# The indexer's scores block by block of queries, and its top search spread between them

## The chip, the cores and the metric

The kernel runs on one core of a Trainium2 chip. The metric is the device time of one execution in microseconds. The kernel before has a median of 2123.04 us over three runs, from 2120.47 to 2123.62.

## The reference, cut to what matters

A hybrid encoder of two layers on 512 tokens of width 1024, in float32. Layer 0's mixer joins two attentions. The differential one ("b") is four heads with two softmaxes each. The sparse one ("a", eight heads) looks, for each query, only at the 128 keys with the highest indexer scores among the admissible ones:

```
idx_logits = einsum('bqhd,bsd->bqhs', iqb, ik) * IDX_DIM ** -0.5
score = einsum('bqh,bqhs->bqs', iwb, relu(idx_logits))     # 8 indexer heads
score = where(key_chunk <= query_chunk, score, -inf)
_, sel = top_k(score, 128)
```

The softmax of "a" then runs over the selected keys. Around the mixer stand feed-forward layers, and behind it attention to 256 memory tokens.

## The kernel before

Products in float32 precision are made of three matmuls of rounded parts (high by high, high by low, low by high), so each operand is split: ScalarE (ACT) writes the rounded high part, VectorE (DVE) or GpSimd (POOL) the low part. TensorE (PE) executes its instructions in the order of the program text. The other engines' order is set by a planner that simulates the time: what is ready and stands first in the program goes first, weight loads and some other parts have high priority, and `issue_after` puts instructions behind a given one on the same engine.

Queries come in four blocks of 128, i = 0 to 3; a block needs the keys up to its own, (i + 1) x 128. Block 0 has only 128 keys and needs no selection.

In `mixer0` two generators are woven together (`weave`, L79): `gemm` yields after each piece of a projection (six matmuls of 512 columns, counted as 1300), `att` yields the gap that it wants before its next step, and pieces are pulled until the gap is used up. So each step of the attention has a known number of pieces behind it. `None` pulls one piece at a time until something is ready. The pieces are six weight chunks w[0] to w[5] of 16 pieces, then 16 of the memory's keys and values (`mem_kv`), then the output projection (`out_proj`). The last one blocks while the head it needs is not done, and before its second half (`fill`) while the attention is going on (`self.attending`, L661).

The steps of `att` in order: the indexer's keys (`index_keys`), the scores (`index_scores`), the first pair of b heads with top search (`attend_diff`), the second pair, the close of its last head (`close_diff`), four pairs of a heads (`attend64`), which read the masks.

- `index_scores` (L948) takes two indexer heads at a time (j = 0 to 3; z = 0, 1). `split_q` (L745) splits all 512 queries of the pair into `qz` (ACT L751, DVE L752). After a gap of I_QK come, for each z, the products of all three blocks (L788; two of 256, two of 384, two of 512 columns, into three banks "pb" of four), three ReLUs on ACT (L963) and three weighted sums into sc[1] to sc[3] on DVE (L966, L968), and a gap of I_S. At the end DVE marks the inadmissible keys (L972).
- `index_top` (L974) finds the highest scores, eight at a time: 16 rounds for each block, a round being MAX8 (L981) and a load and a replacement of these eight by a marker (L982). It is a generator that goes through the three blocks in turn; at the end it writes the masks `mk` (L986).
- `along` (L1308) runs at each gap of the b heads n rounds of the search (TOP_A = 3 in the first pair, TOP_B = 2 in the second pair and in the close), put behind `self.mark`, the last instruction noted by the step.
- `attend_diff` (L881): transposes and splits of q and k (L742, L761, L752, L767), for each of two softmaxes the products (L788), bias and maximum (DVE L801) and exponential (ACT L802); then both are combined into the weights e (DVE L940). The head's rest is done in the next head's gaps: `transpose_p` (PE L813, ACT L816, DVE L817), products with the values (L896), norm (L905 to L914). In `close_diff` it follows without a gap before the transposes.
- `attend64` ends each head likewise with `transpose_p`, a gap of A_PT = 1950 and eight products (L840).

Of the kernel before, what the change touches and what calls it, by code (L numbers as in the profile page):

```python
# [11 lines left out]
F32 = mybir.dt.float32  # L12
F32R = mybir.dt.float32r
BF = mybir.dt.bfloat16
AF = mybir.ActivationFunctionType
OP = mybir.AluOpType
# [3 lines left out]
P = 128  # L20
# [5 lines left out]
QB = S // P  # L26
# [3 lines left out]
INADMISSIBLE = -3.0e38  # L30
TAKEN = -3.4e38
TAKEN_CUT = -3.2e38
MASK = -float(2.0 ** 99)
# [14 lines left out]
I_1 = 1500  # L48
I_2 = 7150
I_3 = 3900  # L50
I_QK = 2600
I_S = 2600
B_N1 = 1300
B_N2 = 1300
C_N = 0
B_END = 3000
TOP_A = 3
TOP_B = 2
X_K = 2600
WS = (2, 3, 0, 1, 1, 2, 1, 2, 0, 0, 3, 2, 1, 1, 0, 3)  # L60
# [46 lines left out]
class Encoder:  # L107
# [837 lines left out]
        for c in self.unfinished():  # L945
            yield B_END if isinstance(c, str) else c

    def index_scores(self, sc, iq, ikt, coef, mp):  # L948

        nc = self.nc  # L950
        for i in range(1, QB):
            sc[i] = mp.tile([P, (i + 1) * P], F32, name="sc%d" % i, tag="sc%d" % i, bufs=1)
        for j in range(4):
            q = self.split_q(iq[j])
            yield I_QK
            for z in (0, 1):
                h = 2 * j + z
                lg = self.logits(q, ikt, z, blocks=range(1, QB))
                for i in range(1, QB):
                    n = (i + 1) * P  # L960
                    bank, o = lg[i]
                    t = mp.tile([P, n], F32, name="rl%d" % i, tag="e%d" % i, bufs=self.ebufs)
                    nc.scalar.activation(t, bank[:, o:o + n], AF.Relu)  # L963
                    c = coef[:, i * 8 + h:i * 8 + h + 1]
                    if h == 0:
                        nc.vector.tensor_scalar(sc[i], t, c, 0.0, op0=OP.mult, op1=OP.add)  # L966
                    else:
                        nc.vector.scalar_tensor_tensor(sc[i], t, c, sc[i], op0=OP.mult, op1=OP.add)  # L968
                yield I_S
        for i in range(1, QB):  # L970
            n = (i + 1) * P
            nc.vector.memset(sc[i][0:64, n - 64:n], INADMISSIBLE)  # L972

    def index_top(self, masks, sc, mp):  # L974

        nc = self.nc
        for _ in range(16):
            for i in range(1, QB):
                yield
                m8 = self.small.tile([P, 8], F32, name="m8", tag="m8", bufs=4)  # L980
                nc.vector.max(m8, sc[i])  # L981
                nc.vector.match_replace(sc[i], m8, sc[i], TAKEN)  # L982
        for i in range(1, QB):
            n = (i + 1) * P
            mk = mp.tile([P, n], BF, name="mk%d" % i, tag="mk%d" % i, bufs=1)
            nc.vector.tensor_scalar(mk, sc[i], TAKEN_CUT, MASK, op0=OP.is_gt, op1=OP.mult)  # L986
            masks[i] = mk

    def index_gemm(self, banks, src, n, xs):

# [11 lines left out]
    def index_keys(self, out, p, epsv, r, mp):  # L1002
        nc = self.nc
        raw = self.xp.tile([72, S], F32, name="ikraw", tag="sq", bufs=2)
        nc.scalar.copy(raw, p[0:72, :])
        yield I_1
        p = self.bank("pb")
        for i in range(QB):
            nc.tensor.transpose(p[:, i * 72:(i + 1) * 72], raw[:, i * P:(i + 1) * P], self.ident[0:72, 0:72])
        nat = self.xp.tile([P, QB * 72], F32, name="iknat", tag="sq", bufs=2)  # L1010
        nc.scalar.copy(nat, p[:, :QB * 72])
        n3 = nat.rearrange("p (i c) -> p i c", c=72)
        sq = self.xp.tile([P, QB * 64], F32, name="iksq", tag="sq", bufs=2)
        s3 = sq.rearrange("p (i c) -> p i c", c=64)
        nc.scalar.activation(s3, n3[:, :, 0:64], AF.Square)
        ss = self.small.tile([P, 4], F32, name="ikss", tag="ss", bufs=4)
        nc.vector.tensor_reduce(ss, s3, axis=AX, op=OP.add)
        nc.vector.scalar_tensor_tensor(ss, ss, 1.0 / 64, epsv, op0=OP.mult, op1=OP.add)
        f = self.small.tile([P, 4], F32, name="ikf", tag="f", bufs=4)
        self.rsqrt(f, ss, 4)  # L1020
        kn = self.xp.tile([P, QB * P], F32, name="ikn", tag="sq", bufs=2)
        k3 = kn.rearrange("p (i c) -> p i c", c=P)
        for z in (0, 1):
            nc.vector.tensor_mul(k3[:, :, z * 64:z * 64 + 64], n3[:, :, 0:64], f.unsqueeze(2).to_broadcast([P, QB, 64]))
        r2 = self.small.tile([P, 4], F32, name="r2", tag="r2")
        nc.vector.scalar_tensor_tensor(r2, r, (64 ** -0.5) * (8 ** -0.5), r, op0=OP.mult, op1=OP.mult)
        coef = self.small.tile([P, 32 + PAD_SMALL], F32, name="coef", tag="coef", bufs=1)[:, :32]
        nc.vector.tensor_mul(coef.rearrange("p (i h) -> p i h", h=8), n3[:, :, 64:72],
                             r2.unsqueeze(2).to_broadcast([P, QB, 8]))
        yield I_2  # L1030
        p = self.bank("pb")
        for i in range(QB):
            nc.tensor.transpose(p[:, i * P:(i + 1) * P], kn[:, i * P:(i + 1) * P], self.ident)
        g = self.col("l0_idx_k_norm")
        kh = mp.tile([P, S], F32R, name="ikh", tag="ikh", bufs=1)
        nc.scalar.activation(kh, p, AF.Copy, scale=g)
        kl = mp.tile([P, S], F32R, name="ikl", tag="ikl", bufs=1)
        nc.vector.scalar_tensor_tensor(kl, p, g, kh.bitcast(F32), op0=OP.mult, op1=OP.subtract)
        ikt = ((kh, kl), (kh, kl))
        out += [ikt, coef]  # L1040
        yield I_3

    def gain_col(self, q, k, scale):
# [283 lines left out]
    def mixer0(self):  # L1327
        pre, I = "l0_", self.I
        with ExitStack() as ctx:
            self.qkbufs, self.vbufs, self.ebufs = 10, 8, 2  # L1330
            mp = self.open_mixer(ctx, pre)
# [45 lines left out]
                yield from self.mix_out(I[pre + "w_out"], list(range(KB)), os, mp)  # L1377

            def att():
                sc, ik = {}, []  # L1380
                yield from self.wait(ready, 0)
                iq, p, v, r = ready[0]
                yield from self.index_keys(ik, p, v, r, mp)
                yield from self.index_scores(sc, iq, *ik, mp)
                yield from self.wait(ready, 1)
                yield B_N1
                masks = {}
                top = self.index_top(masks, sc, mp)
                yield from self.along(self.attend_diff(*ready[1], 0, gb, "bias0", os[0:2], nlam, sub, mp), top, TOP_A)
                yield from self.wait(ready, 2)  # L1390
                yield B_N2
                yield from self.along(self.attend_diff(*ready[2], 2, gb, "bias0", os[2:4], nlam, sub, mp), top, TOP_B)
                yield from self.along(self.close_diff(), top, TOP_B)
                for _ in top:
                    pass
                yield from self.wait(ready, 3)
                yield from self.attend64(*ready[3], 0, 0, ga, "bias0", os[4:6], mp, masks)
                yield from self.wait(ready, 4)
                yield from self.attend64(*ready[4], 0, 2, ga, "bias0", os[6:8], mp, masks)
                yield from self.unfinished()  # L1400

            self.weave(gemm(), att())
            self.xattn(pre, mp)

# [148 lines left out]
```

## Time and profile before

| | |
|---|---|
| median of three runs | 2123.04 us |
| the profiled execution | 2121.99 us, its span 2120.2 us |
| TensorE busy | 98% of the span |
| VectorE / ScalarE / GpSimd busy | 74% / 54% / 17% |
| the chain that ended last | PE 87%, DVE 7%, ACT 2% |

Times are from the start of the span. The indexer's scores lie at 400 to 443 us, the b heads at 443 to 563, the a heads up to 665. [...] "PEclk" is the clock granted to TensorE as a share of full speed.

### The profile page before, as it was taken

The numbers are of one execution on the slowest core, as the hardware profiler recorded it, in microseconds if no ns is written. First come the engines' busy times: TensorE is split into PE (matmuls) and PEld (weight loads), VectorE is DVE, ScalarE is ACT, GpSimd is POOL, SyncE is SP. The second block draws the span as 40 slices with busy tenths as digits, with TensorE's granted clock in tenths as the row PEclk, the third lists the DMA queues.
The fourth block names the chain that finished last, engine by engine and source line by source line (L and its number), as shares of the span: only waits on it lengthen the run. The fifth ranks groups of instructions, "written<-read, shape, count | busy, mean of one in ns | idle before, by whom it ended". The sixth has DMA issues, their size and how long they took to land.

```text
span 2120.2 us, 32519 instructions
## 1 busy us (share of the span) xinstructions
PE 2083.2 (98%) x12830; PEld 1854.7 (87%) x12834; DVE 1572.0 (74%) x2246; ACT 1136.4 (54%) x1701; POOL 366.6 (17%) x319
## 2 busy tenths in 40 slices
PE   8999999999999999999999999999999999999999
PEld 7989898877788889898979899988888878989997
DVE  8858677589876697685789677684668688958676
ACT  6636344466686565362556354344678566625442
POOL 1101003345431120000020000013453022000000
PEclk9999999999999999999999999999999999999999
DMA  7736535222241166464356466334223225636632
GB/s 228 210 118 183 149 92 179 87 75 70 81 133 64 68 189 170 130 188 129 97 165 176 130 170 178 98 121 150 87 82 130 90 70 149 183 117 186 162 98 92
DMA packets 86122, 279.65 MB, mean 132 GB/s; under 512 B 9681, under 2 KB 12881, under 8 KB 85969
## 3 DMA queue, kind: packets, MB, share of 16 engines
q1 hardware_dynamic: 74448, 235.62, 33.6%
q0 software_dynamic: 11520, 41.95, 11.1%
q8 instruction: 101, 1.65, 0.3%
q14 instruction: 53, 0.43, 0.1%
HBM read 271.24 MB, written 6.29 MB: 131 GB/s over the span
## 4 chain that ended last, share of the span: by engine, by line
PE 87%; DVE 7%; ACT 2%; issue 1%; DMA 1%; POOL 1%; SPq 0%; DVEq 0%; POOLq 0%; ACTq 0%
PE ps_pa L445 26%; PE ps_pa L682 11%; PE ps_pb L445 10%; PE ps_pa L580 10%; PE ps_pb L580 10%; PE ps_pa L633 4%; PE ps_pa L319 2%; PE ps_pb L788 2%; PE ps_pa L1227 2%; PE ps_pb L840 1%; PE ps_pa L1079 1%; PE ps_pb L813 1%; PE ps_pb L633 1%; PE ps_pa L998 1%; DVE wl L159 1%
## 5 line engine op out<-in xcount | busy, mean ns | idle before, releaser
L157 ACT ACTIVATE wh<-wf 128x1024 fp32r<-128x1024 f32 (+2 forms) x211 | 215.3, 1021 | 353.8 <-PE ps_pa L580 121.1
L159 DVE TENSOR_TENSOR wl<-wf,wh 128x1024 fp32r<-128x1024 f32 (+2 forms) x169 | 200.1, 1187 | 49.2 <-ACT wh L157 46.5
L424 DVE TENSOR_TENSOR wl<-s,wh 128x1024 fp32r<-128x1024 f32 x108 | 132.5, 1227 | 51.8 <-ACT wh L423 51.8
L423 ACT ACTIVATE wh<-s 128x1024 fp32r<-128x1024 f32 x108 | 114.3, 1059 | 96.1 <-PE ps_pb L445 34.9
L423 ACT ACTIVATE wh<-wf 128x1024 fp32r<-128x1024 f32 x84 | 88.9, 1058 | 112.8 <-PE ps_pa L445 39.3
L502 POOL DMA_DIRECT2D s<-l_ffn_wq x40 | 35.5, 887 | 538.6 <-ACT s L501 538.6
L159 POOL TENSOR_TENSOR wl<-wf,wh 128x1024 fp32r<-128x1024 f32 x42 | 101.8, 2424 | 142.2 <-ACT wh L157 140.6
L682 PE MATMUL ps_pa<-wh,xh 128*128 128x512 f32 x384 | 123.4, 403 | 0.0
L682 PE MATMUL ps_pa<-wh,xl 128*128 128x512 f32 x384 | 119.9, 394 | 0.0
L682 PE MATMUL ps_pa<-wl,xh 128*128 128x512 f32 x384 | 119.4, 392 | 0.0
L475 POOL DMA_DIRECT2D s<-l_ffn_wq x40 | 35.6, 890 | 443.3 <-DMA s<-l_ffn_wq 297.8
L424 DVE TENSOR_TENSOR wl<-wf,wh 128x1024 fp32r<-128x1024 f32 x84 | 102.5, 1220 | 8.0 <-ACT wh L423 5.1
L590 DVE TENSOR_TENSOR dn<-ps_pa,R 128x512 f32<-128x512 f32 x48 | 33.1, 689 | 89.4 <-PE ps_pa L580 89.0
L224 POOL TENSOR_TENSOR acc<-acc,sq 128x512 f32<-128x512 f32 (+1 forms) x37 | 54.1, 1462 | 246.2 <-ACT sq L223 245.0
L580 PE MATMUL ps_pb<-hh,wl 128*128 128x512 f32 x352 | 96.3, 392 | 0.0
L580 PE MATMUL ps_pb<-hh,wh 128*128 128x512 f32 x352 | 96.2, 392 | 0.0
L580 PE MATMUL ps_pb<-hl,wh 128*128 128x512 f32 x352 | 96.2, 392 | 0.0
L580 PE MATMUL ps_pa<-hh,wl 128*128 128x512 f32 x328 | 89.5, 392 | 0.0
L580 PE MATMUL ps_pa<-hl,wh 128*128 128x512 f32 x328 | 89.4, 391 | 0.0
L580 PE MATMUL ps_pa<-hh,wh 128*128 128x512 f32 x328 | 89.4, 391 | 0.0
L590 DVE TENSOR_TENSOR dn<-ps_pb,R 128x512 f32<-128x512 f32 x48 | 33.0, 688 | 73.4 <-PE ps_pb L580 73.0
L682 PEld LDWEIGHTS ps_pa<-wh,xl 128*128 128x128 f32 x384 | 72.7, 189 | 16.1
(377 smaller groups left out, 5950.1 us busy)
## 6 DMA issues: line engine op xcount, KB each, us to landing
wf<-l_ffn_wq SPq DMA_DIRECT2D x120, 512.0 KB, 3.4
s<-l_ffn_wq SPq DMA_DIRECT2D x80, 512.0 KB, 4.5
s<-l_ffn_wq POOLq DMA_DIRECT2D x80, 512.0 KB, 6.7
wf<-l_ffn_wd SPq DMA_DIRECT2D x64, 512.0 KB, 3.8
wf<-l_w_in SPq DMA_DIRECT2D x48, 512.0 KB, 3.2
wf<-l_ffn_wd SPq DMA_DIRECT2D x32, 384.0 KB, 3.0
wf<-l_mem_wkv SPq DMA_DIRECT2D x16, 512.0 KB, 3.2
wf<-l_w_out SPq DMA_DIRECT2D x16, 512.0 KB, 3.2
```

The lines of the kernel that those rows point to most:

```text
L157: self.leading = nc.scalar.activation(wh[:, sl], w[:, sl], AF.Copy)
L159: eng.tensor_sub(wl[:, sl], w[:, sl], wh.bitcast(F32)[:, sl])
L224: self.summed = (eng or nc.gpsimd).tensor_add(acc[:, :n], acc[:, :n], sq[:, :n])
L319: nc.tensor.matmul(p, w[a][:, k * P:(k + 1) * P], xs[k][c], start=k == order[0] and a == c == 0, stop=k == order[-1] and a == 1)
L423: self.leading = nc.scalar.activation(h, t, AF.Copy)
L424: self.parted = nc.vector.tensor_sub(l, t, h.bitcast(F32))
L445: self.nc.tensor.matmul(bank[:, sl], w[a][:, o:o + P], xs[k][b], start=first and z == a == b == k == 0, stop=z == a == 1 and k == KB // 2 - 1,
L580: self.nc.tensor.matmul(bank, w[a][:, j * P:(j + 1) * P], h, start=j == a == e == 0, stop=j == nb - 1 and (a, e) == ops[-1])
L590: nc.vector.tensor_mul(t, bank, f.R)
L633: nc.tensor.matmul(banks[dd], a[:, o:o + P], parts(k)[b], start=k == first and a is wh and b == 0, stop=k == last and a is wl)
L682: nc.tensor.matmul(banks[i], xs[k][a][:, i * P:(i + 1) * P], w[b][:, kk * 512:kk * 512 + 512], start=k == a == b == 0, stop=k == KB - 1 an ...
L788: nc.tensor.matmul(bank[:, o:o + n], a, b[:, :n], start=c == 0, stop=c == len(ops) - 1)
```

## The change

The scores are summed block by block: all eight indexer heads for block 1, then for block 2, then for block 3. Each step (i, j) needs the split of only 128 queries, which `index_query` makes one step ahead, into two buffers for each z. A step's product goes to one bank. The search of block 1 (16 rounds) is run between the sums of block 2, two rounds behind each sum; eight rounds of block 2 run between the sums of block 3, one behind each. What is left (eight rounds of block 2, 16 of block 3) runs as before along the b heads, with TOP_A = 2. The rounds of one block follow one another, where the three blocks took turns; a block's mask is written behind its last round. The gaps of the scores are new.

```diff
-I_QK = 2600
-I_S = 2600
+I_S = ((1300, 1300), (2600, 1300), (1300, 1300))
+I_TOP = (0, 2, 1)
-TOP_A = 3
+TOP_A = 2
...
+    def index_query(self, q, i, mp):
+        nc, out = self.nc, []
+        for z in (0, 1):
+            mine, other = slice(z * 64, z * 64 + 64), slice(64 - z * 64, 128 - z * 64)
+            t = mp.tile([P, P], F32R, name="iqz%d" % z, tag="iqz%d" % z, bufs=2)
+            src = q[mine, i * P:(i + 1) * P]
+            nc.scalar.copy(t[mine, :], src)
+            nc.vector.tensor_sub(t[other, :], src, t.bitcast(F32)[mine, :])
+            out.append(t)
+        return out
+
+    def index_scores(self, masks, iq, ikt, coef, mp):
+        nc = self.nc
+        kh, kl = ikt
+        tops = []
+        todo = [(i, j) for i in range(1, QB) for j in range(4)]
+        nxt = self.index_query(iq[0], 1, mp)
+        for c, (i, j) in enumerate(todo):
+            n = (i + 1) * P
+            if j == 0:
+                sc = mp.tile([P, n], F32, name="sc%d" % i, tag="sc%d" % i, bufs=1)
+            q = nxt
+            if c + 1 < len(todo):
+                i2, j2 = todo[c + 1]
+                nxt = self.index_query(iq[j2], i2, mp)
             for z in (0, 1):
                 h = 2 * j + z
...
+                p = self.bank("pb")
+                for k in (kh, kl):
+                    nc.tensor.matmul(p[:, :n], q[z], k[:, :n], start=k is kh, stop=k is kl)
+                t = mp.tile([P, n], F32, name="rl%d" % i, tag="e%d" % i, bufs=self.ebufs)
+                nc.scalar.activation(t, p[:, :n], AF.Relu)
+                g = coef[:, i * 8 + h:i * 8 + h + 1]
+                if h == 0:
+                    self.mark = nc.vector.tensor_scalar(sc, t, g, 0.0, op0=OP.mult, op1=OP.add)
+                else:
+                    self.mark = nc.vector.scalar_tensor_tensor(sc, t, g, sc, op0=OP.mult, op1=OP.add)
+                with self.tc.issue_after(self.mark.ins):
+                    for _ in range(I_TOP[i - 1]):
+                        next(tops[-1], None)
+                yield I_S[i - 1][z]
+            if j == 3:
+                nc.vector.memset(sc[0:64, n - 64:n], INADMISSIBLE)
+                tops.append(self.index_top(masks, sc, i, mp))
+        self.top = (c for top in tops for c in top)
...
+    def index_top(self, masks, sc, i, mp):
+        nc = self.nc
+        n = (i + 1) * P
+        for c in range(16):
+            m8 = self.small.tile([P, 8], F32, name="m8", tag="m8", bufs=4)
+            nc.vector.max(m8, sc)
+            nc.vector.match_replace(sc, m8, sc, TAKEN)
+            if c == 15:
+                mk = mp.tile([P, n], BF, name="mk%d" % i, tag="mk%d" % i, bufs=1)
+                nc.vector.tensor_scalar(mk, sc, TAKEN_CUT, MASK, op0=OP.is_gt, op1=OP.mult)
+                masks[i] = mk
+            yield
...
             def att():
...
-                yield from self.index_scores(sc, iq, *ik, mp)
+                yield from self.index_scores(masks, iq, *ik, mp)
+                top = self.top
```

## Rows read from the trace of the kernel before

**Rows 1.** The page: busy time, share of the span, instructions.
```profile
PE 2083.2 (98%) x12830; PEld 1854.7 (87%) x12834; DVE 1572.0 (74%) x2246; ACT 1136.4 (54%) x1701; POOL 366.6 (17%) x319
```

**Rows 2.** Busy time by stretch: PE, weight loads, DVE, ACT, POOL, PEclk, DMA share, GB/s.
```profile
400.80:443.40 42.60, 42.60 (x199) 35.81 (x198) 33.85 (x49) 27.60 (x49) 18.06 (x11) 1.00 0.22 75
443.40:563.00 119.60, 111.17 (x548) 92.75 (x547) 110.08 (x298) 70.95 (x144) 55.44 (x35) 0.96 0.21 71
```

**Rows 3.** Waits of PE, 360 to 660 us: total, times, longest.
```profile
PE ps_pb L813 <- DVE e L940: 6.6, 7, 2.9
```

**Rows 4.** Busy time in slices of 10 us, same columns.
```profile
470.00:480.00 10.00, 7.89 (x41) 6.26 (x42) 9.85 (x24) 2.91 (x7) 10.00 (x7) 1.00 0.28 100
...
500.00:510.00 10.00, 7.38 (x24) 5.61 (x25) 9.88 (x21) 2.81 (x5) 7.37 (x6) 0.66 0.17 53
...
540.00:550.00 10.00, 8.21 (x45) 6.82 (x43) 9.99 (x34) 6.49 (x19) 3.41 (x2) 1.00 0.11 36
550.00:560.00 10.00, 8.35 (x36) 6.86 (x37) 8.93 (x23) 3.14 (x6) 2.55 (x2) 0.83 0.11 44
```

**Rows 5.** Busy time in slices of 2 us, same columns.
```profile
504.00:506.00 2.00, 2.00 (x9) 1.90 (x10) 1.92 (x5) 1.31 (x3) 1.28 (x1) 0.50 0.00 0
```

**Rows 6.** Timeline of PE: start, duration, instruction, idle time before.
```profile
404.59 0.63 PE L682 MATMUL ps_pa<-wh,xh 128*128 128x512 f32 x2
...
407.34 0.28 PE L788 MATMUL ps_pb<-ikh,qz 128*128 128x256 f32 x1
...
408.39 0.63 PE L682 MATMUL ps_pa<-wh,xh 128*128 128x512 f32 x2
...
551.11 0.63 PE L813 MATMUL ps_pb<-ident,e 128*128 128x128 f32 x2 [2.89 <-DVE e L940]
...
655.72 0.39 PE L840 MATMUL ps_pb<-pz0h,vp 128*128 128x512 f32 x1
...
657.00 1.25 PE L813 MATMUL ps_pb<-ident,e 128*128 128x128 f32 x10
658.01 0.48 PE L633 MATMUL ps_pa<-oh,wh 128*128 128x512 f32 x1
```

**Rows 7.** Timeline of DVE, same columns.
```profile
403.67 0.69 DVE L693 TENSOR_REDUCE ss<-sq 128x8 f32<-128x512 f32 x1 [0.73 <-ACT sq L691]
404.39 0.23 DVE L696 TENSOR_SCALAR ss<-ss,epsv 128x8 f32<-128x8 f32 x1
...
454.80 1.48 DVE L981 MAX8 m<-sc 128x8 f32<-128x512 f32 x3
...
457.31 0.54 DVE L982 MATCH_REPLACE8 sc<-m,sc 128x384 f32<-128x384 f32 x1
...
547.66 1.01 DVE L981 MAX8 m<-sc 128x8 f32<-128x512 f32 x2
...
550.61 1.94 DVE L940 SCALAR_TENSOR_TENSOR e<-e,w,e 128x128 f32<-128x128 f32 x4
...
659.55 0.55 DVE L817 TENSOR_TENSOR pz2l<-ps_pb,pz2h 128x384 fp32r<-128x384 f32 x1
```

**Rows 8.** Groups of DVE instructions by line: count, busy us, mean ns, idle before.
```profile
L968 DVE SCALAR_TENSOR_TENSOR sc<-rl,coef,sc 128x256 f32<-128x256 f32 (+2 forms) x21 | 15.5, 783 | 3.1 <-ACT rl L963 3.1
L752 DVE TENSOR_TENSOR qz<-qk,qz 64x512 fp32r<-64x512 f32 x6 | 5.8, 971 | 0.2
...
L981 DVE MAX8 m<-sc 128x8 f32<-128x512 f32 x16 | 10.9, 681 | 0.0
L982 DVE MATCH_REPLACE8 sc<-m,sc 128x512 f32<-128x512 f32 x16 | 10.8, 673 | 0.0
L981 DVE MAX8 m<-sc 128x8 f32<-128x256 f32 x16 | 6.6, 412 | 0.1
L982 DVE MATCH_REPLACE8 sc<-m,sc 128x256 f32<-128x256 f32 x16 | 6.5, 406 | 0.0
L982 DVE MATCH_VALUE_LOAD sc<-m,sc 128x8 f32 x48 | 3.7, 76 | 0.1
```

More of the change, by code (lines that the diff above doesn't have):

```diff
@@ L946, in close_diff @@
             yield B_END if isinstance(c, str) else c
-    def index_scores(self, sc, iq, ikt, coef, mp):
-        nc = self.nc
[L951 to L955, printed above, removed]
+    def index_query(self, q, i, mp):
[8 more added lines that the diff above has]
+        return out
@@ L956, in index_scores @@
             for z in (0, 1):
                 h = 2 * j + z
[L958 to L974, printed above, removed]
-        nc = self.nc
[L977 to L987, printed above, removed]
+                p = self.bank("pb")
@@ L1038, in index_keys @@
         nc.vector.scalar_tensor_tensor(kl, p, g, kh.bitcast(F32), op0=OP.mult, op1=OP.subtract)
-        ikt = ((kh, kl), (kh, kl))
-        out += [ikt, coef]
+        out += [(kh, kl), coef]
         yield I_3
@@ L1379, in att @@
             def att():
-                sc, ik = {}, []
+                ik, masks = [], {}
                 yield from self.wait(ready, 0)
@@ L1383, in att @@
                 yield from self.index_keys(ik, p, v, r, mp)
-                yield from self.index_scores(sc, iq, *ik, mp)
+                yield from self.index_scores(masks, iq, *ik, mp)
+                top = self.top
                 yield from self.wait(ready, 1)
                 yield B_N1
-                masks = {}
-                top = self.index_top(masks, sc, mp)
                 yield from self.along(self.attend_diff(*ready[1], 0, gb, "bias0", os[0:2], nlam, sub, mp), top, TOP_A)
```

## The prediction

> **What bounds the kernel now.** Read first the busy times: TensorE (PE) is busy for 2083.2 of 2120.2 us, 98% [rows 1]. A kernel in this state gets shorter only where PE waits or runs at a lower clock, so I look for such places near the change. The busy times by stretch give the two that it touches [rows 2]. While the indexer's scores are summed (400.8 to 443.4 us) PE is busy for all of 42.60 us, at full clock, and VectorE (DVE) for 33.85. In the difference attention behind it (443.4 to 563.0) PE is busy for 111.17 of 119.60 us at a mean clock of 0.96, and DVE for 110.08. That second stretch is short of DVE, and it is where the 48 rounds of the top search (a search for eight maxima, a load of them, a replacement) run today. The list of waits says what PE waits for: the transposes of the weights e wait for DVE's line 940 seven times, 6.6 us together [rows 3]. Slices of 10 us place them [rows 4]: PE is idle for 2.11 us in 470 to 480, 2.62 in 500 to 510, 1.79 and 1.65 in 540 to 560. In 500 to 510 the granted clock falls to 0.66, in 550 to 560 to 0.83. [...] Sum: 8.2 us idle and 5.1 us of clock. These 13.3 us are all that the change can win.
>
> **What it changes for PE.** Nothing in amount: 48 score products as before, of the same 256, 384 and 512 columns, with the same tiles as weights. No DMA is added. Only the place of projection pieces shifts. A piece is six matmuls, (407.34 - 404.59) / 2 = 1.375 us, and six score products take 408.39 - 407.34 = 1.05 us [rows 6]. Before, the gaps of the scores pull 4 x (2 + 2 + 2) = 24 pieces; afterwards 4 x 2 + 4 x 3 + 4 x 2 = 28, so every later step of the attention comes four pieces later in the projections.
>
> **The end of the mixer: +1.3 us.** Counting every gap, the attention pulls 132 pieces today from the first of w[0] on, and 134 can be pulled before out_proj blocks on `attending`. Afterwards it wants 136: the last gap, behind the last head's transposes, gets none of its two. Today those transposes start at 657.00, from 658.01 two pieces follow [rows 6], and DVE has the last lower part written at 659.55 + 0.55 = 660.10 [rows 7]. Without pieces the eight products, 657.00 - 655.72 = 1.28 us at the head before [rows 6], can't end before about 660.6, where 658.0 + 1.28 = 659.3 would be free of waits. Below stands 0 (another wait absorbs it), above 2 x 1.375 = 2.75; I take 1.3. The rest of that head lies beside the four pieces of `fill`.
>
> **DVE in the scores: +1 us, between 0 and 10.4.** Block 1's 16 rounds move in here, each 0.412 + 0.076 + 0.406 = 0.894 us, and eight of block 2's, which lie between that and block 3's 0.681 + 0.076 + 0.673 = 1.430, so 1.16 [rows 8]. That is 14.3 + 9.3 = 23.6 us. The splits of the queries become 24 of 64x128 in place of 8 of 64x512. A search of 512 columns takes 0.269 us longer than one of 256, 1.05 ns for a column; 384 fewer columns take 0.4 off the 0.97 us of a split [rows 8], which leaves 0.3 to 0.57 each: no loss to 6 us, I take 1. With 1 us for the four added pieces' weights DVE has 33.9 + 23.6 + 2 = 59.5 us of work in a stretch that grows to 28 x 1.375 + 8 x 1.05 = 46.9 us. So 12.6 us don't fit. If the searches wait and the rest is served, PE notices nothing (0). If the queue is in program order, the split for step c + 2 stands behind the searches of step c. A step of block 2 then costs DVE 4 x 0.894 for rounds, 2 x 0.783 for sums [rows 8], 0.7 for two splits and, by estimate, 1.0 for the projections' share (33.85 us less 24 sums and 6 splits is 9.2, 0.22 for each us of PE): 6.9 us, beside 4.8 us of PE (three pieces, four products). A step of block 3, with two rounds of 1.16, costs 5.4 beside 3.7. Four of each leave 8.4 + 6.8 = 15.2 us, less one step's lead of 4.8: 10.4. I take a value near the low end, since today's rows show how a round's halves are ordered: the three searches come first, from 454.80, and the replacements after them, that of block 2 at 457.31 [rows 7], not search and replacement of one block in turn. What has to wait for its predecessor lets another through. With one block at a time each half-round waits for the one before, so splits and sums slip between.
>
> **DVE in the difference attention: -2 us, between -8.1 and +4.** Today every gap of the first pair of heads brings one round of each block, three in all, 0.894 + 1.16 + 1.43 = 3.5 us. Afterwards it brings two, of block 2 (2.3 us) and then of block 3 (2.9 us); the first four gaps of the second pair bring 2.9 where 2.3 stood. So the share for each gap falls by 1.2 and 0.6 us and then rises by 0.6, and what didn't fit into the scores is still to be done here. The two waits concerned cost 2.11 and 2.62 + 3.4 = 8.1 us together [rows 4]. All may go; or the 12.6 us left over may deepen them, which I bound by half as much again, 4. The first pair's rounds fall from 24 x 1.16 = 27.9 us to 8 x 1.16 + 8 x 1.43 = 20.7, 7.2 less, against 12.6 left over; but late rounds stop PE only where an instruction that it needs stands behind them. I take a quarter of what is lost there, 2.
>
> The extra order between rounds has a price too. Three independent searches take 1.48 us, where their durations add up to 1.64 (0.412, 0.681 and the mean of the two for the middle one); a dependent pair, reduce and scale, starts 0.03 us after the first one's end (404.39 against 403.67 + 0.69) [rows 7]. A step in a chain so loses some 0.1 us, 48 x 2 x 0.1 = 9.6 us at most if nothing slips between, 0 if something always does. This is inside the bounds above.
>
> [...]
>
> **The closing wait: -4.7 us.** At 551.11 PE has waited 2.89 us for line 940 [rows 6], which starts at 550.61 behind two searches (1.01 us from 547.66) [rows 7] and two replacements. The idle time of this place is 1.79 + 1.65 and its clock 1.7, 5.1 us [rows 4]. Afterwards 8 rounds are left after the first pair's 16, at two a gap: they end in the fourth gap of the second pair, and nothing of them is queued here. The two searches and two replacements, of 512 and 256 columns, are about 1.0 + 0.67 + 0.41 = 2.1 of the 2.95 us between 547.66 and 550.61 [rows 7, 8], and rounds stand ahead of these too. The wait falls to some 0.4 us, at which the clock holds: a wait of 2.11 us in 470 to 480 did not lower it [rows 4]. Bounds: 0 (the leftover arrives here) and 5.1. What is late next is line 1302's, which stays.
>
> ScalarE gets 24 small copies for 8, in a stretch with 27.60 of 42.60 us busy [rows 2]: nothing. The masks come earlier and are used later.
>
> **Sum.** -4.7 - 2 + 1 + 1.3 = -4.4 us. The profiled execution took 2121.99 us (span 2120.2), which gives 2117.6; the median of the runs is 1.05 us higher at 2123.04. On it I predict 2118.6 us.
>
> **Rivals.**
> A, everything smooths: the leftover is served in gaps and all 13.3 us go, less 1.3: -12, 2111. For it: after 563 DVE has slack, and in the chain nothing starves. Against it: DVE's work up to the end of the search is longer than PE's.
> B, the load only moves: the first two waits stay, the scores cost 2, the closing wait keeps half: -2.5 + 2 + 1.3, +0.8, 2123.8. For it: 2.9 us in a gap against 3.5 is little.
> C, slower: in the scores the splits stand behind the searches, 10.4 us, with the closing wait gone and the end paid: 10.4 + 1.3 - 5.1 = +6.6, 2129.6. It decides from the point at which a split starts after PE has used up the step before. For it: 59.5 us of work in 46.9. Against it: the order of the halves [rows 7].
>
> **Chances.** Forecast 0.45, of its own range 2114 to 2122; A 0.20; B 0.21; C 0.14. A measurement of this kernel tells 0.2%, 4.2 us, from no change: faster is below 2118.8, slower above 2127.3. Of the forecast I count half as faster and half as same: faster 0.23 + 0.20 + 0.01 = 0.44, same 0.22 + 0.17 = 0.39 (part of B), slower 0.14 + 0.03 = 0.17. The range, 2110.5 to 2128, takes in A's time and most of C's.
>
> **What will show it.** Right: the wait for line 940 near the close is under 1 us, and the clock there 1.00; PE stays busy in the scores; a wait of about 1.3 us for line 817 stands at the last head, ahead of `fill`. Wrong: PE waits in the scores for the new splits by more than 2 us (C), the slices of the first pair lose more than 8.1 us (B), or the rounds run on into the second head of the second pair, so that the closing wait stays.

## The result: slower by 15 us, outside the range

The changed kernel has a median of 2138.18 us over five runs (2135.74 to 2140.77), against 2123.04: a ratio of 1.0073, 95% interval 1.0058 to 1.0088. Forecast were 2118.6, between 2110.5 and 2128.0. The chance given to slower was 0.17.

The first matmul of the attention to the memory tokens, right behind layer 0's mixer, places the loss. This is that line in the profiled execution before (start of the first and the last, us), and after it the same matmul afterwards (now L1248):

```profile
L1227 PE MATMUL ps_pa<-xh,wh x32: 389/389/478, 679.5 to 701.3; 128*128 128x512 f32 x32
```

```profile
L1248 PE MATMUL ps_pa<-xh,wh x32: 389/389/478, 692.3 to 714.0; 128*128 128x512 f32 x32
```

The mixer takes 12.8 us more, of 17.3 that the profiled execution is longer. Of the rest, 3.4 us come at 1600 to 1800 us, where this execution ran at a mean clock of 0.98, for 1.00 before, with the same waits.

PE's work is what it was. Busy time of the changed kernel on the page [rows 1], then by stretch, up to the end of the search and the second pair and for the rest of the mixer, in the kernel before and in the changed one:

```profile
PE 2089.8 (98%) x12830; PEld 1856.6 (87%) x12834; DVE 1589.6 (74%) x2262; ACT 1137.5 (53%) x1717; POOL 366.9 (17%) x319
```

```profile
380.00:570.00 190.00, 181.57 (x879) 150.98 (x878) 155.19 (x365) 108.31 (x207) 81.15 (x51) 0.97 0.22 75
570.00:690.00 120.00, 117.92 (x621) 97.14 (x624) 88.00 (x182) 88.63 (x177) 39.72 (x36) 1.00 0.31 100
```

```profile
380.00:570.00 190.00, 175.07 (x828) 143.31 (x827) 165.87 (x371) 103.71 (x211) 77.06 (x48) 0.96 0.21 72
570.00:690.00 120.00, 114.79 (x605) 93.75 (x608) 83.47 (x174) 84.89 (x173) 40.72 (x35) 1.00 0.30 97
```

PE has as many matmuls. Of its 6.6 us more of busy time some 5 are, by estimate, the lower clock: a slice's length times what its clock is short of 1.00, summed over slices of the whole span, is 10.2 us, where it was 5.3. DVE is busy for 17.6 us more. PE is idle for 14.93 us up to 570, where it was for 8.43, and for 5.21 behind that, where it was for 2.08. The slices of 10 us that lose most of the changed kernel [rows 4], same columns:

```profile
430.00:440.00 10.00, 6.42 (x24) 4.63 (x23) 9.76 (x21) 4.95 (x10) 2.52 (x1) 0.90 0.27 96
440.00:450.00 10.00, 10.00 (x42) 8.12 (x41) 9.63 (x25) 3.94 (x7) 2.41 (x1) 0.93 0.07 19
...
460.00:470.00 10.00, 7.68 (x38) 6.10 (x37) 9.70 (x26) 7.03 (x13) 4.31 (x3) 1.00 0.15 52
480.00:490.00 10.00, 7.31 (x29) 5.32 (x28) 9.80 (x14) 3.77 (x6) 5.70 (x4) 0.79 0.15 53
490.00:500.00 10.00, 10.00 (x49) 8.59 (x49) 9.80 (x26) 4.11 (x10) 0.59 (x1) 0.87 0.17 54
...
510.00:520.00 10.00, 8.11 (x39) 6.29 (x38) 9.84 (x19) 4.53 (x8) 7.20 (x7) 0.99 0.15 52
520.00:530.00 10.00, 10.00 (x48) 8.58 (x47) 9.80 (x24) 4.04 (x10) 4.53 (x3) 0.84 0.31 107
...
540.00:550.00 10.00, 6.50 (x29) 4.72 (x28) 9.79 (x16) 4.45 (x7) 2.54 (x1) 1.00 0.15 55
...
560.00:570.00 10.00, 9.46 (x50) 7.73 (x49) 5.74 (x21) 5.60 (x16) 3.56 (x3) 1.00 0.24 79
```

The number behind the comma is PE's busy time (what is missing to 10 is idle), the third number behind the comma is DVE's, and the third from the end is PE's clock. DVE is busy for 9.6 to 9.8 us in every one of them but the last, 560 to 570, which is shown for the closing wait. What PE waits for, 360 to 700 us (total, times, longest) [rows 3]:

```profile
PE ps_pa L682 <- DVE vp L727: 7.1, 4, 2.3
PE ps_pa L1100 <- POOL wl L159: 3.2, 2, 2.4
PE ps_pb L788 <- DVE m L801: 2.8, 2, 2.0
PE ps_pb L813 <- DVE e L940: 2.6, 6, 0.7
PE ps_pb L813 <- DVE qz L752: 2.1, 2, 1.3
```

The wait for line 940 is down from 6.6 to 2.6 us. At the head of the list stands one that the kernel before does not have: the projection itself (L682) waits for its own banks, which DVE frees when it writes the low part of the values (L727). Where, in PE's timeline [rows 6]:

```profile
433.73 0.73 PE L682 MATMUL ps_pa<-wh,xh 128*128 128x512 f32 x2 [1.29 <-DVE vp L727]
...
438.14 1.22 PE L682 MATMUL ps_pa<-wh,xh 128*128 128x512 f32 x2 [2.30 <-DVE vp L727]
...
544.92 0.73 PE L682 MATMUL ps_pa<-wh,xh 128*128 128x512 f32 x2 [1.86 <-DVE vp L727]
548.22 0.73 PE L682 MATMUL ps_pa<-wh,xh 128*128 128x512 f32 x2 [1.64 <-DVE vp L727]
...
567.62 0.33 PE L813 MATMUL ps_pb<-ident,e 128*128 128x128 f32 x1 [0.20 <-DVE e L940]
568.28 0.98 PE L813 MATMUL ps_pb<-ident,e 128*128 128x128 f32 x7 [0.34 <-DVE e L940]
```

The last two are the closing wait: 0.54 us in all, at full clock. The first two lie in the scores, the next two beside the weights e of the third head. What DVE does ahead of the second, and GpSimd beside it:

```profile
433.98 0.61 DVE L987 SCALAR_TENSOR_TENSOR sc<-rl,coef,sc 128x384 f32<-128x384 f32 x1
434.62 2.35 DVE L956 TENSOR_TENSOR iqz<-qk,iqz 64x128 fp32r<-64x128 f32 x1
437.00 0.43 DVE L1003 MAX8 m<-sc 128x8 f32<-128x256 f32 x1
437.35 0.73 DVE L727 SCALAR_TENSOR_TENSOR vp<-ps_pa,r,vp 128x512 fp32r<-128x512 f32 x1
```

```profile
434.31 2.52 POOL L159 TENSOR_TENSOR wl<-wf,wh 128x1024 fp32r<-128x1024 f32 x1 [5.75 <-ACT wh L157]
```

A split of 0.28 us takes 2.35: it ends just after GpSimd's low part of a weight, which runs from 434.31 to 436.83. The values stand behind it and a search, and PE behind the values.

The largest such stretch lies further on, in the difference attention. There the four operations of line 940, which take 1.94 us where GpSimd has only a memset of 0.15 us beside them [rows 7], take 5.59 beside three GpSimd operations:

```profile
479.39 5.59 DVE L940 SCALAR_TENSOR_TENSOR e<-e,w,e 128x128 f32<-128x128 f32 x4
```

```profile
479.28 1.04 POOL L700 TENSOR_TENSOR qk<-qk,f 128x512 f32<-128x512 f32 x1
480.28 2.44 POOL L159 TENSOR_TENSOR wl<-wf,wh 128x1024 fp32r<-128x1024 f32 x1
482.68 1.22 POOL L700 TENSOR_TENSOR qk<-qk,f 128x512 f32<-128x512 f32 x1
```

Added up over the whole kernel, the 16 operations of line 940 take 16.0 us, for 11.2 before, and the 32 of line 696 (in the norm of the heads) 16.9, for 12.6. The splits of the queries take hardly more than before: 24 small ones 9.7 us, where eight large ones took 9.4.

Such stretches were in the kernel before, too. Its weighted sums, minimum, median and maximum in ns:

```profile
L968 DVE SCALAR_TENSOR_TENSOR sc<-rl,coef,sc x21: 472/620/2465, 410.1 to 440.2; 128x256 f32<-128x256 f32 x7, 128x384 f32<-128x384 f32 x7, 128x512 f32<-128x512 f32 x7
```

The mean of 783 ns that the prediction used [rows 8] hid it: half of the sums take 0.62 or less, one took 2.465. The mean of 0.97 us for a split hid it too: of those six, half take 0.69 or less and two 1.54. There DVE had time to spare, busy for 33.85 of 42.60 us [rows 2].

### The profile page after: what moved, and what is told of

Read it like the earlier page. It is cut to its first block, busy times and chain, and to the rows that moved or that the text cites. A ratio compares the mean times of both kernels' runs of the same rounds, so it can differ in the third digit from the quotient of the medians.

```text
span 2137.5 us, 32557 instructions
## 1 busy us (share of the span) xinstructions
PE 2089.8 (98%) x12830; PEld 1856.6 (87%) x12834; DVE 1589.6 (74%) x2262; ACT 1137.5 (53%) x1717; POOL 366.9 (17%) x319
## 4 chain that ended last, share of the span: by engine, by line
PE 59%; DVE 3%; ACT 1%; issue 0%; DVEq 0%
PE ps_pa L445 19%; PE ps_pa L580 8%; PE ps_pb L445 8%; PE ps_pb L580 7%; PE ps_pa L682 6%; PE ps_pa L633 2%; PE ps_pa L319 1%; PE ps_pa L1248 1%; PE ps_pb L840 1%; PE ps_pa L1100 1%; PE ps_pb L788 1%; PE ps_pb L813 1%; PE ps_pb L633 1%; DVE wl L159 1%; PE ps_pb L319 1%; DVE xl L207 0%
## 5 line engine op out<-in xcount | busy, mean ns | idle before, releaser
L682 PE MATMUL ps_pa<-wh,xh 128*128 128x512 f32 x384 | 124.5, 406 | 7.1 <-DVE vp L727 7.1
L682 PE MATMUL ps_pa<-wh,xl 128*128 128x512 f32 x384 | 121.3, 398 | 0.0
L682 PE MATMUL ps_pa<-wl,xh 128*128 128x512 f32 x384 | 120.5, 395 | 0.7 <-POOL wl L159 0.7
L682 PEld LDWEIGHTS ps_pa<-wl,xh 128*128 128x128 f32 x384 | 73.2, 191 | 18.0 <-POOL wl L159 1.6
```

The lines of the kernel that those rows point to most:

```text
L682: nc.tensor.matmul(banks[i], xs[k][a][:, i * P:(i + 1) * P], w[b][:, kk * 512:kk * 512 + 512], start=k == a == b == 0, stop=k == KB - 1 an ...
```

## The experiments

Each ratio is against the kernel before, run in the same series on the same chip (medians of before there: 2122.65 to 2124.64 us), with its 95% interval; it differs from the quotient of the medians by up to 0.0007. No interval reaches further than 0.0016 to either side, so a difference of two ratios is uncertain by some 0.0015 to 0.002. Three theories were set against each other first: the place of the rounds on DVE, the chain of dependent half-rounds, and the phase (every later step comes four pieces later).

**e1_chain**, the search alone block after block, same gaps, scores as before.

```diff
-        for _ in range(16):
-            for i in range(1, QB):
+        for i in range(1, QB):
+            for _ in range(16):
```

> The kernel before, its scores untouched; only the top search takes its 48 rounds block after block (16 of block 1, then 16 of block 2, then 16 of block 3) in the same gaps of the difference attention, three and then two a gap, where it took the three blocks in turn. So each half-round depends on the one before. Three theories of the 15 us. Place: what costs is where the rounds stand on VectorE (in the scores and beside the values of w[1], so that the projection's own banks come free late); it expects no change here, 2123 within 4 us. Chain: the dependence itself costs some 0.1 us a step, 96 steps; it expects 2131 or more. Phase: the four pieces by which every later step comes later cost it; it expects 2123 here, as place does.

Measured: 2119.67 us, 0.9977 (0.9966 to 0.9987). No cost of the chain shows; the order gains. The first pair gets lighter rounds, which may be the reason and is not shown to be: line 940 is also less stretched in its first two heads (2.69 and 1.94 us, for 3.68 and 2.71). PE's idle time falls from 2.11 to 0.79 us in 470 to 480 and from 2.62 to under 0.25 in 500 to 510 (there the clock loss of 3.4 goes too); the wide rounds come late, and the closing wait grows to 4.94 us.

**e2_shift**, the phase alone.

```diff
-I_QK = 2600
+I_QK = 3900
```

> The kernel before with I_QK 3900 for 2600: each of the four steps of the scores pulls one piece of the projection more, 28 for 24, so that every later step of the attention comes four pieces later, as in the changed kernel. Scores, splits and search stay as before. Phase expects most of the 15 us here: 2133 or more. Place and chain expect 2123 to 2126 (the last head's lost two pieces, 1.3 us, are in this one too).

Measured: 2132.07 us, 1.0038 (1.0025 to 1.0051). Phase is a cause, worth about half of the loss. Its waits [rows 3 for before], PE's timeline and GpSimd's:

```profile
579.28 0.65 PE L913 MATMUL ps_pb<-ident,orr 128*128 128x128 f32 x4 [1.82 <-POOL orr L244]
...
585.80 0.50 PE L1079 MATMUL ps_pa<-wl,mh 128*128 128x512 f32 x1 [1.97 <-POOL wl L159]
```

```profile
574.50 1.64 POOL L244 TENSOR_TENSOR f<-ss,mhalf 128x8 f32<-128x8 f32 x1
576.10 1.97 POOL L700 TENSOR_TENSOR qk<-qk,f 128x512 f32<-128x512 f32 x1
578.04 1.18 POOL L244 TENSOR_TENSOR orr<-ov,mhalf 128x4 f32<-128x4 f32 x1
579.20 3.23 POOL L244 TENSOR_TENSOR f<-ss,mhalf 128x8 f32<-128x8 f32 x2
...
583.40 2.35 POOL L159 TENSOR_TENSOR wl<-wf,wh 128x1024 fp32r<-128x1024 f32 x1
```

The last head's inverse root (orr) is now queued behind the norm of the heads of w[5], and the memory weights' low part behind both. Before, the root came first:

```profile
566.40 1.01 POOL L244 TENSOR_TENSOR orr<-ov,mhalf 128x4 f32<-128x4 f32 x1 [6.92 <-DVE ov L907]
```

By the gaps, its step followed the 13th of the 16 pieces of w[5] before and follows the first piece of the memory's weights now: four pieces carry it past the end of w[5].

**e3_no_rounds_in_scores**, the changed kernel with the search as before.

```diff
-TOP_A = 2
+TOP_A = 3
...
-                with self.tc.issue_after(self.mark.ins):
-                    for _ in range(I_TOP[i - 1]):
-                        next(tops[-1], None)
```

> The changed kernel with its scores block by block of queries and the 28 pieces, but no round in the scores: the search takes the three blocks in turn in the difference attention, as before (three rounds a gap, then two). Left from the change: the order of the scores, the 24 small splits and the shift by four pieces. Place expects it near the kernel before: 2121 to 2127. Chain expects the same (the turns are back). Phase expects 2133 or more, since the shift is still there.

Measured: 2131.01 us, 1.0035 (1.0022 to 1.0048), the same as e2 and with the same waits. So beside the shift the new order of the scores adds nothing that shows.

**e4_24_pieces**, the changed kernel without the shift.

```diff
-I_S = ((1300, 1300), (2600, 1300), (1300, 1300))
+I_S = ((1300, 1300), (1300, 1300), (1300, 1300))
```

> The changed kernel with I_S (1300, 1300) for block 2 too: 24 pieces in the scores for 28, so no shift; the rounds stay in the scores, in four pieces' less time. Phase expects the time of before, 2123 to 2127. Place expects no gain, 2138, or worse by up to 4 us, since the same VectorE work has 5.5 us less of the scores to stand beside. Chain expects 2138.

Measured: 2130.46 us, 1.0028 (1.0017 to 1.0039): between what phase and place expected. Both count, and add up to the change (0.38 or 0.35, and 0.28, against 0.73%). Among PE's waits, 360 to 700 us, stands now that of rival C, for the new splits:

```profile
PE ps_pb L980 <- DVE iqz L956: 2.2, 2, 1.5
```

**e6_blocks_24**, e4 with its 24 rounds moved out of the scores.

```diff
-I_TOP = (0, 2, 1)
+I_TOP = (0, 0, 0)
-TOP_A = 2
+TOP_A = 3
```

> The changed kernel with 24 pieces in the scores (I_S 1300 throughout) and none of the rounds in them: I_TOP (0, 0, 0), TOP_A 3, the search block after block as in e1_chain. It is e1_chain with the scores in the new order and the 24 small splits, and e4_24_pieces with the 24 rounds moved out of the scores. Theory rounds (the rounds in the scores hold up what stands behind them on VectorE): 2119 to 2122, as e1_chain, some 10 us below e4_24_pieces. Theory splits (the new order of the scores and its small splits cost by themselves): 2126 or more.

Measured: 2123.3 us, 0.9999 (0.9991 to 1.0008). Moving the rounds out of the scores takes off e4's 0.29% (6 us). Against e1 the new order and the small splits cost some 0.2%, so neither theory holds whole.

**e8_low_on_dve**, the changed kernel with the low parts of w[2] on DVE. From 425 to 450 us GpSimd then has nothing to do, and DVE more.

```diff
-WS = (2, 3, 0, 1, 1, 2, ...
+WS = (2, 3, 0, 0, 1, 2, ...
```

> The changed kernel with the four low parts of w[2] computed on VectorE (WS[3] 0 for 1) in place of GpSimd: 4 x 1.21 = 4.8 us more work for VectorE in the scores, but no GpSimd operation beside them. In the changed kernel a split of 0.28 us took 2.35 and sums of 0.6 to 0.7 took up to 2.8 while GpSimd worked on such a low part. Theory collision (those stretched operations are what the values and the splits wait for): faster than the changed kernel by 2 to 5 us, 2133 to 2136. Theory amount (VectorE has too much to do, whatever stands beside it): slower by 2 to 5 us, 2140 to 2143.

Measured: 2131.0 us, 1.0031 (1.0019 to 1.0042), 0.42% (8.9 us) below the changed kernel, with 4.9 us more of low parts on DVE. (The sums that the expectation speaks of took up to 2.38 us, not 2.8.) The same place in its timeline of DVE:

```profile
433.00 0.73 DVE L727 SCALAR_TENSOR_TENSOR vp<-ps_pa,r,vp 128x512 fp32r<-128x512 f32 x1
433.65 0.61 DVE L987 SCALAR_TENSOR_TENSOR sc<-rl,coef,sc 128x384 f32<-128x384 f32 x1
434.29 0.28 DVE L956 TENSOR_TENSOR iqz<-qk,iqz 64x128 fp32r<-64x128 f32 x1
...
434.95 0.74 DVE L727 SCALAR_TENSOR_TENSOR vp<-ps_pa,r,vp 128x512 fp32r<-128x512 f32 x1
```

The split takes 0.28 us, and the second part of the values comes 1.95 us behind the first, where it was 4.41 (432.94 to 437.35). From 420 to 460 us PE loses 0.8 us of idle time and clock, for 5.3; from 460 to 560 it loses 11.6, for 15.9. Only the first of these two gains is traced to operations: behind 460 line 940 is as stretched as ever (15.1 us in all). An edit that moves the low parts could also have won by having the weights ready earlier; but in the changed kernel PE never waits for those of w[2].

**e9_before_low_on_dve**, the control.

> The kernel before with the four low parts of w[2] on VectorE (WS[3] 0 for 1), as e8_low_on_dve did to the changed kernel, where it took some 9 us off. This is its control. Theory collision (the gain of e8 is undoing what the change brought: two-input operations of VectorE on GpSimd's work in a stretch that the change filled up): the kernel before has 8.75 us of VectorE slack in its scores, so nothing to gain, 2121 to 2126. Theory general (the four low parts stand better on VectorE in any case): 2112 to 2118.

Measured: 2123.59 us, 0.9999 (0.9991 to 1.0008). What e8 gained is undoing something that the kernel before does not pay.

**e11_24_low_on_dve**, both undone: e4 with the same WS.

> The changed kernel with both: 24 pieces in its scores (no shift, e4_24_pieces took some 9 us off) and the low parts of w[2] on VectorE (e8_low_on_dve took some 9 us off). If shift and collision are two causes that add up and are the whole loss: 2138 - 9 - 9 = 2120, 2118 to 2124. If the amount of VectorE work is a third cause (the scores are four pieces shorter here and VectorE has 4.8 us more to do): 2127 or more.

Measured: 2123.6 us, 0.9997 (0.9988 to 1.0006). Undoing the two edits, the shift and the low parts of w[2] on GpSimd, takes back the whole loss:

| scores of the changed kernel | low parts of w[2] on GpSimd | on DVE |
|---|---|---|
| 28 pieces | 1.0073 | 1.0031 |
| 24 pieces | 1.0028 | 0.9997 |

The shift is worth 0.34 to 0.45%, the collision with these low parts 0.31 to 0.42%, equal within the noise. What remains of the change is neither faster nor slower than the kernel before, though e1 shows that the order of its rounds alone gains 0.23%.

These are two edits and not two separate mechanisms. All 16 operations of line 940 together, in us:

| before | changed | e8 | e4 | e11 | e2 |
|---|---|---|---|---|---|
| 11.2 | 16.0 | 15.1 | 9.2 | 9.5 | 9.6 |

So in the changed kernel the four pieces bring collisions of their own, at line 940, which go with the pieces (e4, e11) and not with e8's edit. And yet e2, the same shift in the kernel before, costs 0.38% without them. What a shift meets depends on what else has moved.

**e10_chain_low_on_dve** and **e12_chain_all_low_on_dve**, e1 with the low parts of w[2], and of w[2] and w[3], on DVE (WS[3], and WS[3] and WS[4], 0).

> e1_chain (search block after block, scores as before) with the low parts of w[2] on VectorE. Theory collision: as e1_chain, 2118 to 2122. Theory general: 2108 to 2114, and then it beats both kernels.

> e1_chain with the low parts of w[2] and of w[3] on VectorE (WS[3] and WS[4] 0). Those of w[3] are used in the difference attention, where VectorE is busy 9.5 of 10 us: 4 x 1.21 = 4.8 us more work for it there. Theory amount: slower than e10_chain_low_on_dve by 3 to 8 us. Theory collision: within 2 us of it, since what VectorE takes on it gets back from stretched operations.

Measured: 2120.95 us, 0.9983 (0.9974 to 0.9992), and 2128.24 us, 1.0018 (1.0009 to 1.0026). e10 is e1 again. In e12 DVE is too full: PE waits 5.6 us for the last mask (L986). So here taking over GpSimd's work paid only where DVE got back more than it took.

**e5_shift_two**, **e16_shift_two_in_scores**, a shift of two pieces, made in two ways.

```diff
-I_QK = 2600
+I_QK = 3900
-B_N1 = 1300
-B_N2 = 1300
+B_N1 = 0
+B_N2 = 0
```

```diff
-            yield I_QK
+            yield I_QK + 1300 * (j < 2)
```

> The kernel before with I_QK 3900 (four pieces later, as e2_shift) and B_N1 and B_N2 at 0 for 1300: one piece given back ahead of each pair of heads, so that from the second pair on the attention comes two pieces later than before, not four. The square root of the closing head (orr, on GpSimd) then stands ahead of the factors of the heads of w[5] in GpSimd's queue again; in e2_shift it stood behind them and the memory weights' low part behind both. Theory order (the price of the shift is that place in GpSimd's queue, a step and no slope): 2123 to 2126. Theory slope (each piece of shift costs the same, some 2 us): 2128.

> The kernel before with one piece more in the first two steps of the scores only (I_QK 3900 for two of four): a shift by two pieces with every gap of the difference attention as before. The closing head's square root then stands behind one of the four factors of w[5]'s heads, for three in e2_shift. Theory step (what counts is the place in GpSimd's queue): 2122 to 2125. Theory slope (each piece costs the same): 2127 to 2129.

Measured: 2138.36 us, 1.0065 (1.0049 to 1.008), and 2128.45 us, 1.0027 (1.0016 to 1.0037). Both ideas fell for e5: the root stood in front again and PE's idle time behind 570 us was back at 2.8 us, but PE waits longer for line 940. The two pieces taken out ahead of the pairs leave less PE work beside the same rounds, and line 940 itself takes 15.1 us in all (9.6 in e2); which of the two counts more is not shown. The wait:

```profile
PE ps_pb L813 <- DVE e L940: 14.0, 8, 3.9
```

e16 has the time that the slope forecast, but by another way than e2: its loss lies mostly ahead of 570 us (9.8 us idle and 8.5 of clock, for 8.4 and 5.1), and line 940 takes 14.6 us there. So no price for each piece is shown, and the queue behind w[5] is only one of the places where a shift costs.

**e14_shift_kv_low_on_dve**, **e15_before_kv_low_on_dve**, the low parts behind w[5] on DVE, with the shift and without.

```diff
-WS = (2, 3, 0, 1, 1, 2, 1, 2, ...
+WS = (2, 3, 0, 1, 1, 2, 1, 0, ...
```

> e2_shift with the low parts of the weights behind w[5] (the memory's keys and values, and the output projection) on VectorE, WS[7] 0 for 2. In e2_shift PE waits 1.97 us for such a low part and 1.82 us for the closing head's square root, both queued on GpSimd behind the factors of w[5]'s heads; with these waits the clock loses 1.6 us more. Theory GpSimd's queue: most of the 8 us of e2_shift go, 2124 to 2128. Theory elsewhere (the shift costs by another collision before 570 us or at the end): 2130 to 2133.

> The control of e14: the kernel before with WS[7] 0. In it the square root stands ahead of the heads' factors, and PE waits for such a low part only 0.8 us. Both theories: 2121 to 2125. Faster by over 4 us would mean that these low parts stand better on VectorE in any case.

Measured: 2129.04 us, 1.0028 (1.0017 to 1.0038), and 2130.5 us, 1.0033 (1.0021 to 1.0046). In e14 the waits for the low part are gone and that for the root is 0.4 us, but this edit costs 7 us by itself, which the control was not expected to show (2.5 us of it at the norm behind the mixer). With these low parts on DVE the shift costs nothing (1.0028 against 1.0033). That fits GpSimd's queue, and does not prove it, since the edit brings waits of its own.

**e7_big_first**, **e13_sixteen_rounds**, **e17_chain_rounds_behind_close**, **e18_before_rounds_behind_close**, the closing wait. e7 searches the widest block first, with TOP_A = 2 and three rounds a gap in the close; e13 is e11 with I_TOP = (0, 1, 1); e17 (on e1) and e18 (on before) run no round in the last three gaps of the second pair and three a gap in the close.

```diff
+        for i in range(QB - 1, 0, -1):
...
+I_TOP = (0, 1, 1)
...
+                for _ in range(0 if i in skip else n):
+                ... top, TOP_B, (7, 8, 9))
+                ... self.close_diff(), top, 3)
```

> e1_chain with the blocks searched from the widest down (512, 384, 256 columns): two rounds a gap in both pairs, three a gap in the closing steps. The round ahead of the closing wait is then one of 256 columns (0.89 us) for one of 512 (1.43), two of them, and the first pair carries 16 x 1.43 = 22.9 us of rounds for 23.6. Theory load (what counts is how much VectorE work each gap brings; the closing wait of 4.9 us in e1_chain is two wide rounds ahead of line 940): the closing wait falls under 3 us and its clock loss goes, 2113 to 2118. Theory chain (e1_chain gains by the order of halves alone): 2119 to 2121. If the 12 rounds left for the closing steps run on past the first masked logits: 2122 or more, with a wait for a mask.

> e11_24_low_on_dve (both causes undone) with 16 rounds in the scores for 24, I_TOP (0, 1, 1): one round a gap beside the scores of blocks 2 and 3. 16 more stand in the first pair's gaps and 16 in the second's, the last of them ahead of the closing wait's two gaps. The predicted gain was the closing wait, 5.1 us of idle time and clock. If e11 has it and gives it back in its fuller scores: 2117 to 2121 here. If the first pair or the second head of the second pair is then late by as much: 2123 to 2126.

> e1_chain with no round in the last three gaps of the second pair (six rounds of 512 columns, 8.6 us) and three a gap for two in the closing steps behind the closing wait; the masks are used only some 30 us later. In e1_chain the closing wait is 4.9 us and the clock loses 3.4 us at it. Theory load (the wait is the rounds in front of line 940): the wait falls under 1 us, 2112 to 2116, which beats both kernels. Theory collision alone (line 938 took 1.77 us beside GpSimd's low part there, and the rounds matter little): the wait stays over 3 us, 2118 to 2121. If the ten rounds left are then late for the mask or for the first head of 64: 2120 or more with a wait for line 986 or 752.

> The same on the kernel before (blocks in turn): no round in the last three gaps of the second pair, three a gap in the closing steps. Its closing place costs 5.1 us of idle time and clock. Theory load: 2117 to 2120. Theory collision alone: 2122 to 2125.

Measured: e7 2124.38 us, 1.0002 (0.9994 to 1.0011); e13 2123.67, 1.0004 (0.9995 to 1.0013); e17 2129.71, 1.0033 (1.0022 to 1.0043); e18 2125.26, 1.001 (1.0002 to 1.0019). None gains. In e7 and e13 the closing wait stays at 3.92 and 3.62 us; in each a four-column operation ahead of line 940, line 938, runs beside a low part of GpSimd's (e13):

```profile
544.39 1.77 DVE L938 SCALAR_TENSOR_TENSOR es<-rs 128x4 f32<-128x4 f32 x1 [0.35 <-ACT e L802]
```

In e17 the wait falls from 4.94 to 2.74 us in three parts (1.69 + 0.86 + 0.19), and the rounds that were moved are late for their mask:

```profile
544.86 0.63 PE L813 MATMUL ps_pb<-ident,e 128*128 128x128 f32 x2 [1.69 <-DVE e L940]
...
575.43 0.47 PE L788 MATMUL ps_pb<-kz0h,qz 128*128 128x512 f32 x1 [2.17 <-DVE qz L752]
...
581.58 0.58 PE L788 MATMUL ps_pb<-mk,identb 128*128 128x512 bf16 x1 [5.45 <-DVE mk L986]
```

So the closing wait is only in part rounds, and the rounds that e17 took away from it came back as a wait behind it. The versions that beat both kernels are e1, by 0.23% against before, and e10, by 0.17%, the same within the noise.

## Why the prediction was wrong, point by point

Idle time and clock loss of PE (the prediction's 3.4 and 1.7 us of clock are 10 us times what 0.66 and 0.83 are short of 1.00 [rows 4]), summed over slices of 10 us, were 8.4 + 5.1 us up to 570 and 2.1 from there to 690; afterwards 14.9 + 6.8 and 5.2. That is 11.3 us more, of the 12.8 that the mixer lost.

- **The closing wait, -4.7:** right, -4.6 (5.1 less the 0.54 of 560 to 570, clock 1.00). As predicted, no round stands ahead of its line 940 at 566.28. They ended later than the fourth gap of the second pair, though: the last mask is written at 549.81, beside the pair's second head. That is half of a sign that was named for being wrong; the other half, that the closing wait stays, did not come. The gain went into other waits.
- **The scores, +1 (0 to 10.4):** inside its bounds, 5.3 us (430 to 440: 3.58 idle and 1.0 of clock; 440 to 450: 0.7), but by another way. PE waits there for over 2 us, which was to mean rival C. The new splits, which C put in its place, are waited for in e4 (2.2 us); in the changed kernel it is the values of w[1], line 727. That the projection too has its banks freed by DVE was nowhere in the sum.
- **The difference attention, -2 (-8.1 to +4):** the step that failed most. Before, its slices ahead of the close lose 2.11 + 0.27 + 2.62 + 3.4 = 8.4 us; afterwards those from 460 to 560 lose 10.8 idle and 5.1 of clock, 15.9: +7.5. The first pair's slices alone, 460 to 530, lose 12.0, over the 8.1 that was named as a sign of being wrong. The sum counted rounds for each gap and left out what else DVE does there and what stretches it. Of the 10.8 idle, PE waits for line 727 3.5 us, for 752 2.1, for 801 2.0 and for 940 another 2.0: line 940 took 5.59 us at 479, and at 541 two of its operations took 2.89 beside a low part of GpSimd's, with the values of w[4] behind them. The term was also built on a wrong reading. Of the 2.11 us at 470 to 480 before only 0.34 are a wait for line 940; 1.47 are one for line 817. And in front of both that wait and the one at 500 line 940 itself was stretched by GpSimd (3.68 and 2.71 us for 1.94), so not all of these 8.1 us were rounds.
- **The four added pieces:** they were counted only at the mixer's end (+1.3), where there is 0.4 us of wait, for line 845 and not 817. Their price is 0.34 to 0.45% by e2, e4, e8 and e11, 7 to 10 us: the steps of the attention fall on other steps of the projections all along, in GpSimd's queue and DVE's. This term was missing.
- **The order of the half-rounds, 0 to 9.6:** no cost shows (e1 is faster than the kernel before). It was right to leave it out of the sum.
- **DVE's work, 59.5 us in 46.9:** the amount was seen, what stretches it was not. DVE's busy time rose by 17.6 us; by lines, 940 and 696 add 9.1 and the splits 0.3. e8 prices the collisions with w[2]'s four low parts at 8.9 us, and e9 (0.9999) shows them free where DVE has slack; the others are not priced by themselves.
- **PE and ScalarE unchanged:** right (12830 matmuls; 1137.5 us for 1136.4).

Rival C had the right sign, with the wrong victim; that its 6.6 us are the size of one of the two causes (e4's 6 us) is luck. Its time, 2129.6, lay outside the range, which ended at 2128. What stays open: which places make up the shift's 7 to 10 us, since e5, e14 and e16 each trade one wait for another; how e8 gains 4.3 us behind 460; and some 1.5 us of the mixer's 12.8 that the slices don't show.

## What to carry to other kernels

Before an engine that has slack in a stretch is filled up there, look at the minimum, median and maximum of its operations and not at the mean: what GpSimd stretched here, a sum to 2.465 us, cost nothing while DVE had slack (e9, 0.9999). List everything that PE waits for from that engine in the stretch, the banks of the projection among it, not only the step that is edited. And a change in the number of pieces between two steps moves all later steps against the other engines' queues; here four pieces cost as much as the collisions with w[2]'s low parts, by other ways in each kernel.

## What the runs showed of the hardware

Of lines 696, 938, 940, 956 and 987, DVE operations with two inputs in SBUF, eleven started in the changed kernel beside a low part of GpSimd's (2.4 us), and each ended 0.0 to 0.6 us behind it, among them 2.35 us for 0.28 (split), 2.38 for 0.61 (sum of 384 columns, at 426.60), 2.29 for 0.23 (line 696, whose second input is a scalar in SBUF, at 507.01). In e13 line 938 took 1.77, for the 0.16 that it takes in the changed kernel's close, with no low part beside it. GpSimd's products (L700) held up line 940 in the same way: its first operation at 479.39 took 1.08 us, for 0.35, and ended 0.15 behind the product. Searches do run beside low parts: of 48 in the changed kernel the longest took 0.695 us.

```profile
L1003 DVE MAX8 m<-sc x48: 415/558/695, 417.6 to 546.0; 128x8 f32<-128x256 f32 x16, 128x8 f32<-128x384 f32 x16, 128x8 f32<-128x512 f32 x16
```

The values' low part, which reads PSUM, was not held up either: before, one took 0.75 us at 435.88, beside a low part of GpSimd's from 435.35. And GpSimd's inverse roots (L244) held up none of these operations here, though they read two inputs in SBUF: two sums of the changed kernel run at full speed, 0.5 us each, inside one.

```profile
413.81 1.07 DVE L987 SCALAR_TENSOR_TENSOR sc<-rl,coef,sc 128x256 f32<-128x256 f32 x2
```

```profile
413.59 1.68 POOL L244 TENSOR_TENSOR f<-ss,mhalf 128x8 f32<-128x8 f32 x1
```

As an estimate from these lines, a low part that GpSimd computes beside a full DVE can cost DVE some 2.1 us (2.35 - 0.28, 2.29 - 0.23), where DVE takes 1.22 us to compute one itself (4.9 us for the four of e8); e8's gain of 8.9 us with more work on DVE fits that. Why these operations are held up and the others are not, no run shows.
